# Seven block products for gate and up in the first feed-forward layer too, its down product in five groups added by DMA, and a new order of the seven in both layers

## The chip, the cores and the metric

The kernel runs on one core of one Trainium2 chip. TensorE (PE) multiplies, VectorE (DVE), ScalarE (ACT) and GpSimd (POOL) work on tiles in the on-chip memory SBUF and on the accumulators in PSUM (eight banks of 2 KB per partition), and 16 DMA engines move data. DMAs are issued from queues of SyncE (SP), ACT and POOL; only those from POOL's queue add to their destination here (`accum_op=OP.add`). The metric is the device time of one execution in microseconds (us), as the median of several runs. Matmuls are written in float32 in two parts, see below.

## The reference

One inference step of a trunk of two layers over 576 tokens (512 of a prompt, 64 of a sample group), model width 1024. Each layer is a mixer and a gated feed-forward part, both behind an RMS norm and added to the residual x. Layer 0 mixes by dilated sliding-window attention, layer 1 by a diagonal complex state-space scan with a GLU. The part that matters here, the same in both layers:

```python
D_FF = 2816
def swiglu(h, w_gate, w_up, w_down):
    return (jax.nn.silu(h @ w_gate) * (h @ w_up)) @ w_down

h2 = rmsnorm(x, p['norm_ffn'][i])
x = x + swiglu(h2, p['ffn_w_gate'][i], p['ffn_w_up'][i], p['ffn_w_down'][i]).astype(x.dtype)
```

The outputs are the two residual streams, the updated key and value caches (most of which is a copy of the old cache, shifted by 8 positions) and the states of the scan.

## The kernel before

**Tiles.** x lives transposed in SBUF as `xT`: 8 tiles of 128 model rows by 576 tokens. A matmul takes 128 by 128 weights and 288 tokens (HN), half of the tokens. Every float32 operand is split in two, hi (fp32r, a rounded copy made on ACT, tile `whi` or `xgh`) and lo (the rest, a subtraction on DVE, `wlo` or `xgl`), and a product is three matmuls: hi by hi, hi by lo, lo by hi. `split_w` (line 95) splits a weight tile of 512 KB (`raw`, four k-tiles by 256 columns), `mm6` (line 105) issues the six matmuls of three terms and two token halves.

**Stages in order of time.** The qkv projection with attention over the caches (to about 397 us of the span); the output projection (`wo_phase`), four chunks of 256 columns, each followed by the residual addition on DVE and by `Norm.add`, which splits the new tile for the next layer part and adds its squares to `ssum` (ACT squares, POOL adds); the first feed-forward layer (`ffn`, 423 to 868 us); the state-space part (`ssm_phase`) with its GLU (to about 1065 us); the second feed-forward layer (`ffn_last`).

**First feed-forward layer, `ffn`.** 11 units of 256 columns. A unit computes its gate chunk directly, 2 halves of columns x 8 k-tiles x 6 matmuls, multiplies by the norm's factor `r` on DVE (L1078), takes silu on ACT (L1079), multiplies by r again on POOL (L1080); then the same for up, and the product of both (L1085) is split to `hh` and `hl` (L175, L176). After 4, 8 and 11 units (`THIRDS`) the down product of these units is computed in four chunks of 256 columns of the model width, and DVE adds it into `xT` (L1091). After each chunk of weights `tick()` runs a piece of `fill`: `ssm_setup` is a generator that computes the constants of the state-space layer (powers, tables, masks; mostly DVE and POOL with some transposes on PE) and writes them to DRAM scratch; its last pieces load the first four sets back.

**Second feed-forward layer, `ffn_last`.** Gate and up of a unit are taken together as one product with a 2 by 2 block structure: weights a11 to a22 (row halves by k halves, prepared on the host in `w_gu`; each block is 128 partitions by 4 k-tiles by 256 columns), activations b11 to b22 (k halves by token halves). Seven products of sums of blocks replace eight (line 1097):

```python
PRODUCTS = (("a11", "b11"), ("s1", "t1"), ("a12", "b21"), ("s2", "t2"), ("s3", "t3"), ("a22", "t4"), ("s4", "b22"))
```

s1 and s3 are made by DMA: a block is loaded through SP's queue, and a second one added to it from POOL's queue (`plus`, L1127). s2 is s1 + a11 on DVE (L1156), and becomes s4 by one more `plus`. The t operands are sums of the b, made with their splits in `Norm7.add` (lines 235 to 256) during the GLU: seven hi and seven lo parts per pair of tiles of x, four sums on DVE (L244, L249, L251, L253). The products accumulate in three pairs of banks (x, y and z in `products`); between two products that use the same bank, ACT or DVE copies the partial sum out (`ended`, L1178 `cp`, L1182 `cq`). Weights of the next unit are fetched when s3 of the present one is split.

**Queues.** SP issues loads and cache copies in program order. The copies of the old cache into the outputs (`shifts`, 88 of about 1 MB, DRAM to DRAM) are paid out by `pace`: each weight load in the feed-forward layers with `rate=RF` = 1.0 adds one copy. The order of instructions on each engine is set by the framework's scheduler from the program order; where `keep_in_program_order` or `issue_after` stands, by hand.

## Time and profile before

| what | us |
| --- | --- |
| median of 3 runs (1469.40 to 1473.09) | 1471.54 |
| the profiled execution | 1472.93 |
| its span in the trace | 1471.1 |
| output projection, PE's last matmul ends about | 423 |
| first feed-forward layer | 423 to 868 |
| second feed-forward layer | 1066 to 1471 |

The mean granted clock of TensorE over the span is 0.994. A row of the group view reads: line, engine, operation, output <- inputs, shapes, count | busy time in us, mean of one in ns | idle time of the engine before it, and what ended that. Matmuls are pipelined, so their own durations (about 295 ns) overlap; how far apart they follow is read from the busy time of a stretch and the number of matmuls in it. A row of the view by stage gives busy time and number of instructions of PE, PE's weight loads, DVE, ACT and POOL, then the granted clock, the mean busy share of the 16 DMA engines and GB/s. [...]

### The profile page before, as it was taken

To read this page: it belongs to the slowest core of one execution; us is meant where nothing else is said; L and a number is where in the kernel's file an instruction comes from. 1 tells how busy PE (TensorE), PEld (TensorE's weight loads), DVE (VectorE), ACT (ScalarE), POOL (GpSimd) and SP (SyncE) were. 2 spreads that over 40 slices of the span, in tenths; PEclk is the share of its full clock that TensorE was granted. 3 is DMA by queue.
4 is the path that set the end of the run, shared out by engine and by line. 5 is a ranking of instruction groups with operands and counts; after the bars stand their busy time and mean duration, and the time that the engine had idled before them with its cause. 6 is when DMAs were issued, how large, how long until landed. Compare 5 with 4: busy or idle time off the path is not lost. (4 is left out here: it accounts for less than half of the span.)

```text
span 1471.1 us, 30038 instructions
## 1 busy us (share of the span) xinstructions
PE 1432.1 (97%) x12398; PEld 1341.1 (91%) x12398; DVE 1000.9 (68%) x1696; ACT 596.0 (41%) x962; POOL 334.6 (23%) x410
## 2 busy tenths in 40 slices
PE   9999999999999999999999999699999999999998
PEld 7888777777899999999999999699999999999998
DVE  5898989745578653687777567856587646755772
ACT  4534455465462221223123363434365324532541
POOL 2022131320031066156245330131010001100110
PEclk9999999999999999999999999899999999999999
DMA  7566798999897757888979857964267767775532
GB/s 243 207 232 234 224 306 278 347 307 330 301 298 257 264 216 270 300 298 313 318 269 319 290 178 227 275 181 130 86 169 190 242 216 184 184 244 156 146 110 63
DMA packets 181048, 345.73 MB, mean 235 GB/s; under 512 B 40720, under 2 KB 116304, under 8 KB 179504
## 3 DMA queue, kind: packets, MB, share of 16 engines
q1 hardware_dynamic: 168176, 309.00, 61.4%
q0 software_dynamic: 9968, 32.12, 9.8%
q10 hardware_dynamic: 2768, 2.70, 0.6%
q8 instruction: 97, 1.59, 0.4%
q14 instruction: 39, 0.32, 0.1%
HBM read 312.29 MB, written 118.78 MB: 293 GB/s over the span
## 5 line engine op out<-in xcount | busy, mean ns | idle before, releaser
L108 PE MATMUL acc<-xgh,wlo 128*128 128x288 f32 x1056 | 227.6, 297 | 3.4 <-DVE wlo L100 3.4
L108 PE MATMUL acc<-xgh,whi 128*128 128x288 f32 x1056 | 229.5, 299 | 0.0
L108 PE MATMUL acc<-xgl,whi 128*128 128x288 f32 x1056 | 227.3, 297 | 0.0
L99 ACT ACTIVATE whi<-raw 128x1024 fp32r<-128x1024 f32 x98 | 102.0, 1041 | 242.8 <-PE acc L108 193.9
L1171 PE MATMUL bank<-xoh,whi 128*128 128x288 f32 x616 | 182.5, 296 | 4.2 <-ACT cq L1182 2.8
L1171 PE MATMUL bank<-xoh,wlo 128*128 128x288 f32 x616 | 181.7, 295 | 0.2 <-DVE wlo L1113 0.2
L1171 PE MATMUL bank<-xol,whi 128*128 128x288 f32 x616 | 181.7, 295 | 0.0
L108 PEld LDWEIGHTS acc<-xgh,wlo 128*128 128x128 f32 x1056 | 170.6, 189 | 4.0 <-DVE wlo L100 3.9
L108 PEld LDWEIGHTS acc<-xgh,whi 128*128 128x128 f32 x1056 | 170.3, 189 | 1.8 <-issue 1.2
L108 PEld LDWEIGHTS acc<-xgl,whi 128*128 128x128 f32 x1056 | 170.5, 189 | 0.1
L100 DVE TENSOR_TENSOR wlo<-raw,whi 128x1024 fp32r<-128x1024 f32 x98 | 124.7, 1272 | 67.3 <-ACT whi L99 66.3
L1171 PEld LDWEIGHTS bank<-xoh,whi 128*128 128x128 f32 x616 | 115.7, 188 | 6.1 <-ACT cq L1182 4.4
L1113 DVE TENSOR_TENSOR wlo<-raw,whi 128x1024 fp32r<-128x1024 f32 (+1 forms) x57 | 70.7, 1241 | 73.3 <-ACT whi L1112 73.3
L384 PE MATMUL acc<-whi,xh 128*128 128x512 f32 x288 | 118.7, 414 | 1.6 <-ACT xh L324 1.5
L1171 PEld LDWEIGHTS bank<-xoh,wlo 128*128 128x128 f32 x616 | 115.8, 188 | 0.6 <-DVE wlo L1113 0.6
L1171 PEld LDWEIGHTS bank<-xol,whi 128*128 128x128 f32 x616 | 115.7, 188 | 0.1
L1112 ACT ACTIVATE whi<-raw 128x1024 fp32r<-128x1024 f32 (+1 forms) x57 | 58.4, 1029 | 136.6 <-DMA raw<-ffn_w_down 52.1
L384 PE MATMUL acc<-wlo,xh 128*128 128x512 f32 x288 | 112.2, 391 | 0.0
L384 PE MATMUL acc<-whi,xl 128*128 128x512 f32 x288 | 111.5, 393 | 0.0
L108 PE MATMUL acc<-hh,whi 128*128 128x288 f32 x352 | 76.2, 297 | 0.0
L1080 POOL TENSOR_TENSOR gt<-gt,rstd 128x576 f32<-128x576 f32 x22 | 39.4, 1794 | 160.5 <-ACT gt L1079 160.4
L1127 POOL DMA_DIRECT2D s<-w_gu x22 | 19.4, 883 | 247.3 <-DMA s<-w_gu 145.5
(445 smaller groups left out, 3142.5 us busy)
## 6 DMA issues: line engine op xcount, KB each, us to landing
o_kv_s<-cache_kv_w SPq DMA_DIRECT2D x64, 1020.0 KB, 7.7
kc<-cache_kv_w SPq DMA_DIRECT2D x100, 512.0 KB, 6.9
raw<-ffn_w_down SPq DMA_DIRECT2D x40, 512.0 KB, 3.8
raw<-w_qkv SPq DMA_DIRECT2D x36, 512.0 KB, 7.0
raw<-w_gu SPq DMA_DIRECT2D x33, 512.0 KB, 3.4
kc<-qscr SPq DMA_DIRECT2D x32, 512.0 KB, 6.1
o_kv_s<-cache_kv_w SPq DMA_DIRECT2D x16, 1008.0 KB, 7.5
raw<-ffn_w_gate SPq DMA_DIRECT2D x22, 512.0 KB, 5.1
```

What stands on the lines that cost most here:

```text
L99: s.activation(hi, raw, AF.Copy)
L100: mark[0] = v.tensor_tensor(lo, raw, hi.bitcast(F32), OP.subtract)
L108: pem[0] = te.matmul(ps[:, c, :HN], w, x[:, c * HN:(c + 1) * HN], start=first and i == 0, stop=last and i == 2)
L384: ins = nc.tensor.matmul(*a, **kw)
L1080: g.tensor_tensor(t, t, nin.r, OP.mult)
L1112: s.activation(hi, raw, AF.Copy)
L1113: v.tensor_tensor(lo, raw, hi.bitcast(F32), OP.subtract)
L1127: g.dma_start(fl(t), block(c, m, k), accum_op=OP.add)
L1171: tc.keep_in_program_order(te.matmul(acc[q][:, :HN], a[:, k, i * 128:(i + 1) * 128], nin.x[x, k][b], skip_group_check=n != "a12", start=n ...
```

## The change

- `ffn_last` becomes `ffn` for both layers (argument `layer`), so the first layer too computes gate and up in seven block products. The host now prepares `w_gu` for both layers. The first layer has 6 PSUM banks for it (the other two stay with `aux` for the set-up), one buffer each for s1 and s3 instead of two (`1 + layer`), s2 in a `raw` buffer, and 4 for `hh`/`hl`. For the first unit its s2 is made by DMA.
- The norm ahead of the first layer (`n0`) becomes a `Norm7`: `wo_phase` makes seven split operands per pair of tiles; those of the last pair come after all residual additions. The norm's last step is computed after the first three k-tiles of three products, and partly on POOL.
- The new order of the seven, in both layers: a11, a12, s2, s1, s3, s4, a22. s1's partial sum is copied out by ACT; s3 and s4 are added to such copies by DVE.
- The first layer's down product is computed in five groups of units, (2, 2, 2, 2, 3); the first four are computed after the first product of the next unit, evicted by ACT, and added to `xT` by a DMA from POOL's queue. The last group is added on DVE.
- The cache copies are paid out otherwise: 11 in the attention part (`SHIFTS`), 0.2 per split and 0.5 per down load in the first layer, some 16 in the GLU, 0.3 and 0.5 in the second layer.
- `ssm_setup` is cut into more and smaller pieces; several copies and the masks go from DVE to ACT, one step of powers from POOL to DVE, and the loads of its first four sets of constants move into `ssm_phase`, onto SP's queue.
- The attention output's hi parts (`ath`) lie in four buffers of `kst`, and pools are opened and closed at other places.

```diff
-RF = 1.0
+SHIFTS = (4, 5, 6, 7, 10, 11, 15, 16, 17, 18, 19)
+RF = 0.5
...
-            v.tensor_tensor(t, self.r, self.r, OP.mult)
-            v.tensor_tensor(t, t, m, OP.mult)
+            e = v if self.perm else g
+            e.tensor_tensor(t, self.r, self.r, OP.mult)
+            e.tensor_tensor(t, t, m, OP.mult)
...
-                v.scalar_tensor_tensor(self.r, t, 1.5, self.r, op0=OP.add, op1=OP.mult)
+                g.tensor_scalar(t, t, 1.5, None, op0=OP.add)
+                g.tensor_tensor(self.r, t, self.r, OP.mult)
...
-    n0 = Norm(1)
+    n0 = Norm7(1, xo)
...
-            n0.add(2 * c + m)
+            if c < 3:
+                n0.add(f)
+    n0.add(6)
+    n0.add(7)
...
+PRODUCTS = (("a11", "b11"), ("a12", "b21"), ("s2", "t2"), ("s1", "t1"), ("s3", "t3"), ("s4", "b22"), ("a22", "t4"))
+GROUPS = (((0, 2), (2, 4), (4, 6), (6, 8), (8, 11)), ((0, 4), (4, 8), (8, 11)))
+PACE = (0.2, 0.3)
+FETCH = ("a11", "s1", "a12", "s3", "a22")
...
+    bk = es.enter_context(tc.tile_pool(name=f"bk{layer}", bufs=8 if layer else 6, space=PSUM))
...
+    def fetch(c, n):
+        if n[0] == "a":
+            W[c][n] = load(c, "12".index(n[1]), "12".index(n[2]), ring, "raw", 4)
+        else:
+            W[c][n] = load(c, 1, 0, r7, n, 1 + layer)
+            plus(W[c][n], c, *{"s1": (1, 1), "s3": (0, 0)}[n])
...
+            if n == "s3":
+                if c + 1 < 11:
+                    fetch(c + 1, "a11")
+                if tail:
+                    fetch_down(*tail, 0)
+                if c + 1 < 11:
+                    for i in FETCH[1:] if not tail else ("s1", "s3"):
+                        fetch(c + 1, i)
...
+            pace(PACE[layer])
+            tick()
...
+            elif n in ("s1", "s2"):
+                s.activation(t[i][n == "s1"][:, 1], p, AF.Copy)
+            elif n in ("s3", "s4"):
+                d = t[i][n == "s3"][:, 1]
+                v.tensor_tensor(d, p, d, OP.add)
...
+        for n, x in rest:
+            ready(n)
+            for i in range(2):
+                products(n, x, i, range(4))
+            if n == "a11" and mid is not None:
+                down(*mid, False)
...
+                if not end:
+                    y = wk.tile([128, 2, HN], F32, name=f"{'gu'[c % 2]}t{m}")
+                    for q in range(2):
+                        if layer:
                             v.tensor_tensor(y[:, q], ps[m][q][:, :HN], nin.r[:, q], OP.mult)
+                        else:
+                            s.activation(y[:, q], ps[m][q][:, :HN], AF.Copy)
+                    if layer:
                         v.tensor_tensor(xv, y, xv, OP.add)
+                    else:
+                        g.dma_start(xT[:, f, :], y.rearrange("p a b -> p (a b)"), accum_op=OP.add)
+                    continue
...
-                tt = wk.tile([128, 8, 16, 8], F32, name="wo")
-                v.tensor_tensor(tt.rearrange("p g c t -> p t (g c)"), st, tmask[:, :, None].to_broadcast([128, 8, 128]), OP.mult)
+                for t in range(8):
+                    s.activation(tt.rearrange("p g c t -> p t (g c)")[:, t], st[:, t], AF.Copy, scale=tmask[:, t:t + 1])
...
+    consts_in(0, nc.sync)
     stage1(0)
     fetch1(2)
+    consts_in(1, nc.sync)
     stage1(1)
...
+            with tc.issue_after(L["mark"][0].ins):
+                L["pace"]((0.0, 1.75, 1.75, 1.0 if c0 >= D else 0.0)[c0 % D // 256])
```

599 lines of the change are left out of this document (319 added, 280 removed).

## The prediction

> **What bounds the kernel now.** I read the page's busy times first, then the list of what TensorE (PE) waits for, then the busy times by stage.
>
> ```profile
> span 1471.1 us, 30038 instructions
> PE 1432.1 (97%) x12398; PEld 1341.1 (91%) x12398; DVE 1000.9 (68%) x1696; ACT 596.0 (41%) x962; POOL 334.6 (23%) x410
> ...
> PE acc L1646 <- DMA U<-u_scr: 11.6, 2, 10.9
> ...
> PE bank L1171 <- ACT cq L1182: 2.8, 6, 0.8
> PE bank L1171 <- ACT sq L198: 1.4, 1, 1.4
> ```
>
> PE is busy for 97% of the span, and of its waits by far the largest is 11.6 us in stage 2 of the state-space part; the seven products of the second layer wait 2.8 and 1.4 us. So the kernel is as long as its queue of matmuls, and a matmul removed in a stage without waits is time removed, provided that nothing else becomes late there. In the next view each row is a stretch: busy time and instructions of PE, weight loads, DVE, ACT, POOL, then granted clock, DMA share, GB/s.
>
> ```profile
> 403.00:423.00 20.00, 20.00 (x152) 20.00 (x151) 17.41 (x33) 12.32 (x18) 7.91 (x6) 1.00 1.01 264
> 423.00:868.00 445.00, 442.55 (x3411) 438.98 (x3410) 303.60 (x566) 127.70 (x142) 179.41 (x148) 1.00 0.80 284
> 630.00:680.00 50.00, 50.00 (x401) 49.26 (x400) 41.58 (x64) 14.92 (x17) 27.06 (x16) 1.00 0.96 336
> ...
> 1090.00:1156.00 66.00, 65.36 (x487) 64.51 (x486) 46.52 (x60) 37.23 (x57) 7.77 (x9) 1.00 0.79 204
> ...
> 1252.00:1274.00 22.00, 22.00 (x168) 21.98 (x168) 15.75 (x20) 12.13 (x19) 2.59 (x3) 1.00 0.79 195
> ```
>
> 423 to 868 is the whole first feed-forward layer: PE 442.55 of 445 us. The last row holds exactly one unit of the second layer (seven products, 168 matmuls) without a gap: 22.00 / 168 = 131 ns per matmul of 288 columns. That is the price of a matmul in what follows.
>
> **The saving.** Gate and up of one unit of 256 columns take 192 matmuls now (2 matrices x 2 halves of columns x 8 k-tiles x 3 terms x 2 halves of tokens), and 7 x 2 x 4 x 3 = 168 in the new form. 24 x 11 units = 264 matmuls, x 131 ns = **-34.6 us**. The down product keeps its 1056 matmuls whatever its groups, and the set-up of the state-space layer, which runs in the gaps of this stage, keeps its transposes. In the second layer the new order puts two products instead of one between two that share a bank, so that the copy of an accumulator has 6.3 us of matmuls (48 x 131 ns) over it in place of 3.1 us: the 2.8 us of waits for cq should go, **-2.8 us**, at worst 0.
>
> **The late start.** The block products need seven split operands per pair of 128-row tiles in place of two wider ones, made in the output projection, which is short. Rows: DVE's residual adds, its low halves and sums, the weight split, and one of the sums that ran beside POOL.
>
> ```profile
> L1038 DVE TENSOR_TENSOR xT<-acc,xr 128x288 f32<-128x288 f32 (+1 forms) x16 | 9.2, 620 | 1.2 <-DMA xr<-x_scr 1.2
> L1038 DVE TENSOR_TENSOR xT<-acc,xr x16: 548/622/698, 403.4 to 423.7; 128x288 f32<-128x288 f32 x8, 128x224 f32<-128x224 f32 x8
> L100 DVE TENSOR_TENSOR wlo<-raw,whi 128x1024 fp32r<-128x1024 f32 x98 | 124.7, 1272 | 67.3 <-ACT whi L99 66.3
> L232 DVE SCALAR_TENSOR_TENSOR xol<-S,xoh 128x288 fp32r<-128x288 f32 x16 | 6.6, 444 | 0.0
> L232 DVE SCALAR_TENSOR_TENSOR xol<-xT,gm,xoh 128x288 fp32r<-128x288 f32 x12 | 6.1, 511 | 1.8 <-ACT xoh L231 1.8
> L199 POOL TENSOR_TENSOR ssum<-ssum,sq 128x576 f32<-128x576 f32 x21 | 35.7, 1701 | 137.1 <-ACT sq L198 137.1
> L1039 DVE TENSOR_TENSOR xT<-acc,xr x8: 209/218/237, 404.4 to 424.2; 128x64 f32<-128x64 f32 x8
> L249 DVE SCALAR_TENSOR_TENSOR S<-xT,gm,S x4: 1501/1676/1676, 994.2 to 1070.1; 128x288 f32<-128x288 f32 x4
> L251 DVE SCALAR_TENSOR_TENSOR S<-xT,gm,S x4: 504/506/508, 995.6 to 1071.7; 128x288 f32<-128x288 f32 x4
> ```
>
> From the first add, at 403.4 us, DVE has: adds 9.2 + 8 x 0.218 = 10.9 us; five weight splits (two of the projection, three of the first unit) x 1.27 = 6.4; low halves 16 x 0.41 + 12 x 0.51 = 12.7; sixteen sums x 0.506 = 8.1. That is 38 us. Durations overlap a little at their ends (the busy time of sixteen L232 is 6.6 us, not 7.1), so 34 us is possible; with seven POOL additions over it (L199), each lengthening one two-input instruction by 1.676 - 0.506 = 1.2 us as in L249, 46 us. DVE is therefore done at 437 to 450 us, and the operands of the last pair that the early products need come some 3 us before. PE ends the projection near 423, and has 54 matmuls of the first three pairs and the norm's two sums over, about 8 us, so until 431. Stall 434 - 431 = 3 us to 447 - 431 = 16 us; I take **+9 us**, the middle. Now there is no stall here (20.00 of 20 us busy, 403 to 423).
>
> [...]
>
> ```profile
> 940.00:950.00 10.00, 3.86 (x64) 3.89 (x66) 5.00 (x10) 2.40 (x8) 0.00 (x0) 0.50 1.04 293
> ```
>
> A PE gap lowers the granted clock here: it is 0.50 in the stretch of the 10.9 us wait. I price this at nothing beyond the gap itself, within the bounds above. [...]
>
> **The rest of the first layer.** Three resources get fuller. Rows of DVE and of the DMA queues, the first six in the stretch 423 to 868, the next four in three units of the second layer (1090 to 1156).
>
> ```profile
> L100 DVE TENSOR_TENSOR wlo<-raw,whi 128x1024 fp32r<-128x1024 f32 (+1 forms) x69 | 87.1, 1262 | 41.2 <-ACT whi L99 40.3
> L1562 DVE TENSOR_TENSOR wo<-st,tmask 128x1024 f32<-128x1024 f32 x8 | 17.7, 2218 | 0.3
> L1439 DVE COPY cwd<-cw 128x128 f32<-128x128 f32 x16 | 4.8, 297 | 4.8 <-PE aux L1440 4.8
> q1 hardware_dynamic: 53665, 125.78, 79.9%
> o_kv_s<-cache_kv_w SPq DMA_DIRECT2D x59, 1020.0 KB, 7.7
> o_kv_s<-cache_kv_w SPq DMA_DIRECT2D x4, 1008.0 KB, 9.6
> ...
> q0 software_dynamic: 1243, 4.50, 39.9%
> q1 hardware_dynamic: 2570, 8.90, 38.6%
> s<-w_gu SPq DMA_DIRECT2D x6, 512.0 KB, 4.9
> s<-w_gu POOLq DMA_DIRECT2D x6, 512.0 KB, 6.4
> ```
> ```profile
> L1078 DVE TENSOR_TENSOR gt<-acc,rstd 128x576 f32<-128x576 f32 x22 | 16.3, 750 | 6.4 <-PE acc L108 6.3
> L1085 DVE TENSOR_TENSOR ut<-acc,gt 128x576 f32<-128x576 f32 x22 | 16.6, 754 | 9.6 <-PE acc L108 8.9
> L1091 DVE TENSOR_TENSOR xT<-acc,xT 128x576 f32<-128x576 f32 x24 | 18.1, 756 | 22.1 <-PE acc L108 22.1
> L1200 DVE SCALAR_TENSOR_TENSOR ut<-ut,gt 128x576 f32<-128x576 f32 x22 | 16.5, 750 | 3.9 <-ACT ut L1184 2.3 <-POOL gt L1197 1.3
> L1194 DVE SCALAR_TENSOR_TENSOR gt<-gt,rstd 128x576 f32<-128x576 f32 x22 | 18.0, 818 | 0.1
> L1188 DVE TENSOR_TENSOR gt<-bank,cp 128x288 f32<-128x288 f32 x11 | 5.0, 450 | 0.0
> L1156 DVE TENSOR_TENSOR S<-s,raw 128x1024 f32<-128x1024 f32 x11 | 13.4, 1215 | 0.0
> L1112 ACT ACTIVATE whi<-S 128x1024 fp32r<-128x1024 f32 x22 | 23.4, 1061 | 21.0 <-PE bank L1171 11.9 <-DMA S<-w_gu 8.7 <-DVE S L1156 0.3
> ```
>
> DVE: 303.6 us now. Gone: 44 of the 69 splits (55.5), L1078 and L1085 (32.9), two thirds of L1091 (12, the down sums go by DMA, their eviction to ACT), the masks L1562 (17.7, to ACT) and some 70 small copies like L1439's that move to ACT or vanish (x 0.297, some 20). New: 77 splits x 1.26 = 97; ten S sums 12; 66 evictions with an addition x 0.45 = 30; 44 products with the norm, 18.0 + 16.5 = 35; some 8 us of powers taken from POOL and 14 us that the late start leaves behind 423. 165 + 196 = **361 us** in a stage of 445 - 34.6 = 410 us: 88%, against 68% now and 83% in the densest stretch quoted (41.58 of 50 us, with PE at 50.00).
>
> DMA: a plain MB costs 355.6 / 125.78 = 2.83 us of all 16 engines, an accumulating one 26.3 / 4.50 = 5.85 us; a unit of the second layer costs (26.3 + 25.5 - 2.9 for one cache copy) / 3 = 16.3 us. Now 355.6 us. Gone: 44 loads of gate and up (23.1 MB, 65 us; a few lie before 423, as the first unit's will), some 36 of 63 cache copies (they go to the attention part, the GLU and the second layer: 106 us), the constants' 7.3 MB (21). New: 11 x 16.3 = 179, and 32 additions of 0.295 MB into xT x 5.85 = 55 (this form is not in the trace; at the plain price it is 27). **370 to 398 us** over 410: 90 to 97%, against 80% now and 96% in the densest 50 us.
>
> So PE, DVE and DMA have nearly equal work. What hides the new work is only depth: weights split one or two products (3.1 us each) ahead. The longest chain is that of s1: load 4.9 us, POOL's issue and the accumulating load 6.4, the S sum 1.2 (L1156), the split on ACT and DVE 1.06 + 1.26, together 15 us; there are five products (15.7 us) plus the lead between the product that starts it and the one that needs S. It fits, by little; the second layer's order of before leaves the same chain four products, and PE's waits show nothing of it. A fetch or addition queued on POOL behind one that waits holds all of POOL's arithmetic, and those behind SP's cache copies (7.7 us to land) come later too. Cost: 0 if it goes as in the second layer (there 4.2 us of waits in eleven units with DVE at 46.5 / 66 = 70%), up to 25 us if DVE can do no more than its densest 83% (361 / 0.83 = 435 us, less 410). I take **+8 us**, nearer to the second layer because the same loop ran there. Cache copies moved into the attention part (11 x 3 us of DMA in a stretch with room) and the GLU: 0 to 3, **+1 us**.
>
> ```profile
> 40.00:170.00 130.00, 129.56 (x626) 105.48 (x625) 118.35 (x154) 58.33 (x89) 21.56 (x40) 1.00 0.62 214
> 990.00:1062.00 72.00, 72.00 (x544) 71.95 (x543) 44.99 (x59) 29.64 (x48) 7.23 (x5) 1.00 0.40 119
> ```
>
> The room is in these rows: DMA 62% and 40% busy. The GLU takes about 16 copies x 3 us in 72 us, which fills it. The wait for U (11.6 us) comes from the order on SP's queue, which now carries the constants' loads as well; it may vanish or double, 0 +-12, I take 0.
>
> **Sum**, against the profiled execution's own 1472.9 us (span 1471.1 and 1.8 around it): -34.6 - 2.8 + 9 + 8 + 1 = -19.4, so 1453.5. That execution is 1.4 us over the median of the three runs (1471.5), so **1452 us** as a median. This kernel's times are told from no change at about 0.3%, 4.4 us.
>
> **Rivals.**
> - *Nothing new is late* (0.12): operands are made in the order in which PE needs them, stall 3, later stalls 0: 1472.9 - 37.4 + 3 - 1.4 = 1437 us. For it: PE 50.00 of 50 with DVE at 83% and DMA at 96%. Against: all of it at once, for 400 us.
> - *DVE becomes the bound of the first layer* (0.20): 435 us there plus 3 of the late start not counted in it, in place of 445: -7, with the second layer's order -2.8, +1, or 1463 us; with worse bunching up to 1471. Half of this is within 0.3%. PE then does less work, as the change says, and waits for the difference.
> - *DMA becomes the bound* (0.15), the slower end: the stage's 398 us at a mean share of 0.85, which lies between today's 0.80 and the densest 0.96, take 468 us, 23 more than now: 1472.9 + 23 - 2.8 - 1.4 = 1492 us. It decides from a mean share below 398 / 448 = 0.89. Against it: stretches of 0.96 and 1.01 above, with PE full.
> - The forecast (1443 to 1463): 0.53.
>
> Faster by over 0.3%: 0.53 + 0.12 + 0.11 = 0.76; within: 0.09; slower: 0.15. The range 1438 to 1480 leaves out half of the first rival and most of the third.
>
> **What would show it.** PE should have some 264 matmuls fewer; the first layer should last about 427 us. The late start shows as a wait of PE for DVE's or ACT's operands at 423 to 445 us; DVE as bound shows as many PE waits for split weights (wlo); DMA as bound as ACT's split waiting for raw or S with the DMA row at 9 throughout. The waits for cq in the second layer should be gone. The forecast is wrong if the late start exceeds 16 us, if waits inside the first layer sum to more than 25 us, or if the wait for U moves by more than its size.

## The result: 4.5% slower, and the profile after

| what | before | after |
| --- | --- | --- |
| median, runs of both beside each other, us | 1472.32 (1469.4 to 1475.51, 4 runs) | 1538.75 (1534.01 to 1544.52, 4 runs) |
| ratio of the times | | 1.0452, 95% interval 1.041 to 1.0495 |
| span of the profiled execution, us | 1471.1 | 1537.2 |

The change makes the kernel 66 us slower, where the prediction had 20 us faster and a range that ended at 1480. The page of the kernel after, in its first two parts:

```profile
span 1537.2 us, 30220 instructions
PE 1431.4 (93%) x12134; PEld 1330.9 (87%) x12134; DVE 1082.0 (70%) x1767; ACT 715.9 (47%) x1293; POOL 390.3 (25%) x461
...
PEclk9999999999979999999989999989999999999999
```

PE has 12398 - 12134 = 264 matmuls fewer, as the arithmetic of the seven products says, and yet it is busy for as long as before (1432.1 us then). So two things must have happened: matmuls became slower, and idle time appeared (97% of the span became 93%). The clock row (slices of 38.4 us) has its 7 and its first 8 in the first layer. The view by stage says where. First the kernel after, in stretches that begin and end where a stage does (columns as in the prediction), then the stages behind the first layer in the kernel before:

```profile
427.70:924.50 496.80, 435.63 (x3132) 424.10 (x3131) 380.41 (x633) 249.04 (x473) 226.86 (x194) 0.93 0.81 225
...
924.40:1129.50 205.10, 186.58 (x1931) 183.05 (x1931) 133.05 (x200) 83.09 (x151) 34.02 (x47) 0.96 0.87 285
1129.50:1531.20 401.70, 395.28 (x2941) 390.77 (x2942) 246.32 (x323) 168.44 (x251) 44.37 (x41) 1.00 0.68 208
```

```profile
867.20:1066.80 199.60, 184.70 (x1922) 181.26 (x1921) 133.31 (x198) 83.67 (x157) 33.61 (x47) 0.97 0.58 172
...
1066.80:1465.20 398.40, 394.62 (x2943) 390.10 (x2943) 245.80 (x326) 170.53 (x251) 36.81 (x37) 1.00 0.62 175
```

The first layer grows from 445.0 to 496.8 us: +51.8 of the 66. The rest is small: the output projection ends at 427.7 instead of about 423 (+4.7), the state-space part and GLU take about 6 us more, the second layer 3.3 us more, although it got the better order.

The 51.8 us can be split further. Before, PE's idle time in the stage was 445.00 - 442.55 = 2.5 us; now it is 496.80 - 435.63 = 61.2 us, **58.7 us more idle**. At the matmul price of before PE would have been busy for 442.55 - 34.6 = 408 us; it is busy for 435.6, so there are **27.7 us of slow matmuls**. 58.7 + 27.7 - 34.6 = 51.8. The saving is there in full, and is outweighed two and a half times.

What ended the idle time shows in PE's waits in this stage (us in total, times, longest):

```profile
PE bank L1251 <- DVE hl L186: 10.7, 6, 2.9
PE bank L1188 <- DVE wlo L1101: 9.9, 8, 2.8
PE bank L1188 <- ACT whi L1100: 7.8, 2, 5.5
PE bank L1251 <- ACT hh L185: 7.1, 3, 4.3
PE bank L1188 <- ACT xoh L243: 6.3, 1, 6.3
PE aux L1629 <- ACT wo L1621: 6.2, 3, 3.9
PE bank L1188 <- DVE gt L1202: 4.9, 2, 3.4
PE bank L1188 <- DVE ut L1202: 4.8, 2, 3.5
```

L1188 are the seven products, L1251 the down product. No single wait carries the loss. PE waits for DVE and for ACT by turns, for split weights, evictions and the down product's operands, 2 to 6 us at a time; before, the same layer had one such wait:

```profile
PE acc L108 <- DVE wlo L100: 2.5, 1, 2.5
```

About 16 us of the idle time after lie in the first unit (6.3 us ahead of its first product, 5.5 ahead of its last, four small ones), the other 45 inside the layer.

How one such wait comes about is seen in the timeline of DVE (start, duration, instruction, in brackets the idle time ahead of it):

```profile
543.37 0.44 DVE L1202 TENSOR_TENSOR gt<-bank,gt 128x288 f32<-128x288 f32 x1
550.81 1.22 DVE L1159 TENSOR_TENSOR raw<-s,raw 128x1024 f32<-128x1024 f32 x1 [7.00 <-issue]
551.96 0.45 DVE L1202 TENSOR_TENSOR ut<-bank,ut 128x288 f32<-128x288 f32 x1
```

L1159 is the sum s2 = s1 + a11. It stood at the head of DVE's queue for 7.00 us, because the transfer that adds the second block to s1, issued at 541.0, landed only at 550.7. The eviction L1202 behind it did not pass it: its inputs were ready by 549.0, and it began at 551.96, 3 us later. PE ran out at the same place:

```profile
552.46 0.40 PE L1188 MATMUL bank<-xoh,whi 128*128 128x288 f32 x1 [3.50 <-DVE ut L1202]
```

The transfers, issue to landing, in the first layer of the kernel after:

```profile
s<-w_gu POOLq DMA_DIRECT2D x20, 512.0 KB, 9.6
s<-w_gu SPq DMA_DIRECT2D x19, 512.0 KB, 5.3
```

An accumulating load takes 9.6 us here, 6.4 in the three units of before's second layer that the prediction used. With L1159 at a mean of 1.52 us and wlo at 1.44 (before 1.26), the chain of s1 is 5.3 + 9.6 + 1.5 + 1.06 + 1.44 = 19 us, not 15, over five products that last 15.7: it does not fit.

The slow matmuls follow the gaps. Stretches of about 2 us around a wait of 2.14 us that ended at 819.26, and around one of 1.63 us that ended at 656.84:

```profile
815.00:817.00 2.00, 2.00 (x16) 1.89 (x15) 1.53 (x2) 0.00 (x0) 2.00 (x2) 1.00 1.06 295
817.00:819.20 2.20, 0.12 (x1) 0.00 (x0) 0.46 (x1) 1.02 (x2) 2.20 (x3) 1.00 0.90 321
819.20:821.00 1.80, 1.74 (x19) 1.33 (x20) 0.82 (x1) 1.23 (x3) 0.97 (x3) 0.51 1.08 200
821.00:823.00 2.00, 2.00 (x11) 2.00 (x11) 1.59 (x2) 0.00 (x0) 1.92 (x3) 0.59 1.00 317
823.00:825.00 2.00, 2.00 (x18) 2.00 (x16) 0.00 (x0) 0.74 (x2) 0.99 (x1) 1.00 0.91 134
...
656.80:659.00 2.20, 2.16 (x16) 2.16 (x17) 2.20 (x4) 0.09 (x1) 0.00 (x0) 1.00 0.97 171
```

Behind the longer one the granted clock (third number from the end) is 0.5 from 819.2 to 822.6, 3.4 us; behind the shorter one it stays 1.00. So this gap of 2 us cost nearly 4. Length alone does not decide, though. Behind a longer wait, of 2.76 us, the clock stays 1.00:

```profile
670.71 0.40 PE L1188 MATMUL bank<-xoh,wlo 128*128 128x288 f32 x1 [2.76 <-DVE wlo L1101]
```

```profile
667.90:670.70 2.80, 0.05 (x1) 0.00 (x0) 2.80 (x2) 0.00 (x0) 2.72 (x3) 1.00 1.03 274
670.70:675.90 5.20, 4.95 (x47) 4.52 (x48) 5.17 (x6) 2.85 (x5) 5.04 (x3) 1.00 1.02 346
```

What does is seen in the trace's record of the granted clock. All its changes in this kernel fall on one grid of 3.41 us. Among the stretches of this grid at full clock, each with 1.83 us or more of idle PE was followed by one at half the clock, and none with 1.67 us or less was; full clock came back only after a stretch with at most 0.33 us idle. In the kernel before, whose changes lie on such a grid too, 2.42 us did and 1.84 us did not. The wait of 2.14 us lies almost wholly in one stretch (2.11 us of it); the one of 2.76 us is divided by a line of the grid at 669.0 into 1.1 and 1.7 us.

### The profile page after: what moved, and what is told of

Its sections match the earlier page's. It is cut to its first block, busy times and chain, and to the rows that moved or that the text cites. A ratio compares the mean times of both kernels' runs of the same rounds, so it can differ in the third digit from the quotient of the medians.

```text
span 1537.2 us, 30220 instructions
## 1 busy us (share of the span) xinstructions
PE 1431.4 (93%) x12134; PEld 1330.9 (87%) x12134; DVE 1082.0 (70%) x1767; ACT 715.9 (47%) x1293; POOL 390.3 (25%) x461
## 5 line engine op out<-in xcount | busy, mean ns | idle before, releaser
L1188 PE MATMUL bank<-xoh,whi 128*128 128x288 f32 x1232 | 373.5, 303 | 29.3 <-ACT whi L1100 9.3
L1188 PE MATMUL bank<-xoh,wlo 128*128 128x288 f32 x1232 | 372.3, 302 | 12.7 <-DVE wlo L1101 12.6
L1188 PE MATMUL bank<-xol,whi 128*128 128x288 f32 x1232 | 370.8, 301 | 1.1 <-DVE xol L244 1.1
L1188 PEld LDWEIGHTS bank<-xoh,whi 128*128 128x128 f32 x1232 | 238.9, 194 | 33.5 <-ACT whi L1100 9.9
L1101 DVE TENSOR_TENSOR wlo<-raw,whi 128x1024 fp32r<-128x1024 f32 (+1 forms) x136 | 182.0, 1339 | 103.2 <-ACT whi L1100 103.0
L1188 PEld LDWEIGHTS bank<-xoh,wlo 128*128 128x128 f32 x1232 | 238.5, 194 | 16.9 <-DVE wlo L1101 16.8
L1188 PEld LDWEIGHTS bank<-xol,whi 128*128 128x128 f32 x1232 | 238.6, 194 | 1.5 <-DVE xol L244 1.4
L1251 PE MATMUL bank<-hl,whi 128*128 128x288 f32 x352 | 85.8, 309 | 10.7 <-DVE hl L186 10.7
L1251 PE MATMUL bank<-hh,whi 128*128 128x288 f32 x352 | 84.7, 309 | 7.2 <-ACT hh L185 7.1
L1251 PE MATMUL bank<-hh,wlo 128*128 128x288 f32 x352 | 83.9, 306 | 0.0
L109 PE MATMUL acc<-xgl,whi 128*128 128x288 f32 x352 | 75.6, 295 | 2.3 <-DVE xgl L1694 2.3
L109 PE MATMUL acc<-xgh,whi 128*128 128x288 f32 x352 | 75.2, 298 | 0.9 <-ACT whi L100 0.9
L1251 PE MATMUL bank<-xgh,wlo 128*128 128x288 f32 x352 | 75.5, 295 | 0.5 <-DVE wlo L1101 0.5
L109 PE MATMUL acc<-xgh,wlo 128*128 128x288 f32 x352 | 75.2, 295 | 0.3 <-DVE wlo L101 0.2
L1251 PE MATMUL bank<-xgh,whi 128*128 128x288 f32 x352 | 75.3, 295 | 0.0
L1251 PE MATMUL bank<-xgl,whi 128*128 128x288 f32 x352 | 75.0, 294 | 0.0
## 6 DMA issues: line engine op xcount, KB each, us to landing
o_kv_s<-cache_kv_w SPq DMA_DIRECT2D x64, 1020.0 KB, 10.5
```

Source lines behind the costliest of these rows:

```text
L109: pem[0] = te.matmul(ps[:, c, :HN], w, x[:, c * HN:(c + 1) * HN], start=first and i == 0, stop=last and i == 2)
L1101: v.tensor_tensor(lo, raw, hi.bitcast(F32), OP.subtract)
L1188: L["pem"][0] = tc.keep_in_program_order(te.matmul(acc[q][:, :HN], a[:, k, i * 128:(i + 1) * 128], nin.x[x, k][b], skip_group_check=n != " ...
L1251: L["pem"][0] = te.matmul(ps[m][q][:, :HN], w, x[:, q * HN:(q + 1) * HN], start=a + k + j == 0, stop=a + k == len(ks) - 1 and j == 2)
```

## The experiments

Three theories at first. **A**: the set-up of the state-space layer, which runs beside the units, makes the units late on shared queues. **B**: the transfers are late, by the single buffer for s1 or by the cache copies beside them. **C**: the down sums that go by DMA from POOL's queue hold POOL. "Stage" is from the first of the seven products of the first layer to its last down product: 434.0 to 924.0, 490.0 us, in the kernel after. Except for the two repairs (4 runs) and the new order alone (12 runs) each kernel below ran once. The four runs of the whole change lie 10.5 us apart, so a difference of 6 or 8 us is a single reading, not more.

**All set-up ahead of the units.**

```diff
-    n1 = ffn(nc, tc, A, L, 0, n0, ssm, sp)
+    for _ in ssm:
+        pass
+    n1 = ffn(nc, tc, A, L, 0, n0, iter(()), sp)
```

> The whole set-up of the state-space layer runs before the first unit of the first feed-forward layer, none of it beside the units. Read by stage, not by total (the set-up alone then stands in the open and costs 100 us or more). Changed kernel: first product to last down matmul of the first layer 434 to 924, 490 us, of which PE idles some 55 and loses some 28 to a lower clock. Theory A (the set-up's arithmetic on POOL, ACT and DVE beside the units is what makes their operands late): the stage falls to 381 us of matmuls plus 5 to 25, 386 to 406 us, with PE waits under 20 us. Theory B (the loads and accumulating loads of the units' own weights are late, through one buffer for s1 and the cache copies): the stage stays above 440 us, with the waits for split weights as many as before. Theory C (the down sums by DMA on POOL's queue hold the others): above 440 us as well, waits at the group boundaries unchanged.

1675.85 us beside 1473.85 for before, since nothing covers the set-up now; but the stage itself takes 429.0 us. Its waits:

```profile
PE bank L1190 <- DVE ut L1204: 18.2, 4, 6.3
PE bank L1190 <- ACT cp L1197: 10.2, 1, 10.2
PE aux L1646 <- DVE kk L1638: 0.7, 1, 0.7
PE bank L1253 <- DVE hl L186: 0.3, 1, 0.3
```

The waits for hl, hh, wlo and wo are gone. What is left is one gap at the start and four at the sum of s1. The accumulating loads of s1 and s3 take 10.8 us even here, so it is not the set-up that makes them slow. So set-up matters, and is not all.

**No cache copies in the first layer** (they go to the second).

```diff
-PACE = (0.2, 0.3)
+PACE = (0.2, 0.65)
...
-            pace(PACE[layer])
+            pace(PACE[layer] if layer else 0.0)
```

The down weights' rate becomes 0 in the first layer as well.

> No cache copies are paid out in the first feed-forward layer; the second layer takes them (0.65 per split instead of 0.3). Theory B with the copies as its cause: loads land sooner (5.3 to about 4 us, accumulating ones 9.6 to about 7), the stage falls from 490 to 430 to 450 us and the total by 40 to 60 us. Theory A or C: the stage stays within 15 us of 490, total within 15 us of 1538 (the second layer may lose a few us).

The stage takes 481.3 us, 9 less, where theory B with the copies as its cause had 40 to 60; the accumulating loads land in 7.7 us. But the whole is 1582.5 us, 44 slower than the change: the second layer, which now has the copies, went from 402 to 458 us. There, one row of the transfers and one of PE's waits:

```profile
S<-w_gu POOLq DMA_DIRECT2D x11, 512.0 KB, 15.3
```

```profile
PE bank L1188 <- ACT whi L1100: 40.4, 9, 8.0
```

The addition that turns S2 into S4 lands in 15.3 us there, against 9.4 in the kernel after and 5.5 in the version with the new order alone (below), and PE waits for its split. The share of DMA is 0.76 in this layer as a mean, but the mean hides when. While ten of these eleven additions were under way (11.8 to 19.8 us each) it was 0.80 to 1.01; it was 0.62 during the eleventh, which landed in 5.4 us. One of the ten and the eleventh:

```profile
1293.60:1309.90 16.30, 15.94 (x121) 15.70 (x119) 7.88 (x12) 4.71 (x7) 0.87 (x1) 1.00 0.96 298
1512.10:1517.50 5.40, 5.40 (x43) 5.40 (x42) 4.17 (x6) 3.17 (x5) 2.32 (x2) 1.00 0.62 97
```

So the cache copies were no filler without a price: the single transfer on the chain was late while the share was 0.80 or more, whatever the mean of 0.76 says.

**Down sums on DVE instead of by DMA.**

```diff
-                        g.dma_start(xT[:, f, :], y.rearrange("p a b -> p (a b)"), accum_op=OP.add)
+                        v.tensor_tensor(xv, y, xv, OP.add)
```

> The down sums of the first four groups are added into the residual by DVE from the evicted copy (32 additions of about 0.75 us) instead of by DMA from POOL's queue. Theory C: the stage falls from 490 to 450 us or less, accumulating weight loads land in about 7 us. Theories A and B: within 15 us of 490, or longer by up to 24 us because DVE has more to do.

1537.28 us, stage 488.9: no difference, though DVE is busy for 20 us more (393.88 of 488.9):

```profile
431.10:920.00 488.90, 436.38 (x3131) 425.18 (x3131) 393.88 (x651) 245.06 (x468) 214.06 (x158) 0.92 0.70 206
```

Theory C falls, and this is a first sign that DVE's busy time isn't what counts. Nor is it the sum of the transfers: the DMA share falls from 0.81 to 0.70, which is 55 us less, and the stage is as long.

**A second buffer for s1 in the first layer.**

```diff
-            W[c][n] = load(c, 1, 0, r7, n, 1 + layer)
+            W[c][n] = load(c, 1, 0, r7, n, 2 if layer or n == "s1" else 1)
```

Room for it comes from laying short-lived tiles of the set-up over each other.

> Two buffers for s1 in the first layer instead of one (room made by laying three small tiles of the set-up over others). Theory B with the single buffer as its cause: DVE no longer waits 5 to 7 us for s1 ahead of the S sum, the stage falls from 490 to 440 to 460 us, total by 30 to 50 us. Theories A and C: within 15 us of 490.

1529.68 us, stage 478.2, 12 less. The waits for gt and ut fall from 9.7 to 2.0 us; hl (11.4), wlo (11.1), wo (7.0) and hh (6.8) stay. The 7.8 us of waits for whi are gone as well, which are not waits at the sum: 5.5 of them stood ahead of the first unit's last product, where the addition that makes s4 landed 12.3 us after its issue at 456.30, and now lands 5.4 us after 452.32. The waits for cp rise to 4.6. So the 12 us are not the chain of s1 alone.

**Both: set-up ahead and two buffers for s1.**

> All set-up ahead of the units, as in the run of that kind, and a second buffer for the block S1 in the first layer. There the layer's products and down product took 429 us against about 381 us of matmuls at full clock: 28.9 us idle, 18.2 of them in four waits for an eviction that stood on DVE behind a sum waiting for S1, and about 19 us of slow matmuls. Theory B (the chain over the one S1 buffer is what is left, and the slow matmuls come with its gaps): the four waits go, and with them about two thirds of the slow matmuls; the stage takes 400 to 412 us. Theory A (set-up alone, S1 only waits for something else): within 6 us of 429. Rival D (the accumulating loads are late whatever the buffers are, because the DMA engines are full, 81% there): 418 to 429 us, the waits moved to other blocks.

The stage takes 395.9 us, less than theory B hoped for. The row of its stretch, of the kind shown above:

```profile
634.30:1030.20 395.90, 391.89 (x2909) 390.81 (x2909) 240.94 (x279) 201.62 (x330) 117.32 (x103) 0.99 0.85 235
```

All four waits at the sum are gone, with the matmuls' slowness. It also corrects the price in the expectation: full-clock matmuls are about 390 us here, not 381, so that the set-up's own are 408 - 390 = 18 us. Now the parts can be priced. The second buffer is worth 12 us beside the set-up and 33 without it (429.0 to 395.9). With two buffers, the set-up costs 478.2 - 395.9 = 82 us, 18 of them its own matmuls: **64 us are interplay**. And PE is at 99% here with DMA at a mean share of 0.85, so such a share need not hold the products up. This stage is without the set-up's transfers, however. With them it has 0.81 x 490 = 397 us of DMA, which would be 0.96 of the 414 us that are hoped for; whether the stage could be as short as that with all its transfers, no run here shows.

**What of the set-up does it?** Four kernels on this. In the first, POOL's arithmetic for the table V is left out, and zeros are stored in its place.

```diff
-                for i, (a, b, op) in enumerate(((c1, c2, OP.add), (c2, c1, OP.subtract))):
-                    g.tensor_tensor(vv[:, i], a, p1r, OP.mult)
-                    g.tensor_tensor(vt_, b, p1i, OP.mult)
+                for i in range(2):
+                    g.memset(vv[:, i], 0.0)
                     yield
-                    g.tensor_tensor(vv[:, i], vv[:, i], vt_, op)
```

> Leaves out the six POOL operations that compute the recurrence's V table in each of its eight steps (48 operations, 79 us of POOL in the first layer) and stores zeros of the same size in its place. Theory L (POOL and DVE exclude each other: the differences wlo average 1.44 us in the first layer against 1.24 before, and single ones took 5.19 us beside these operations): wlo falls to 1.30 us or less, the first layer's stage from 490 to 465 to 478 us. Rival (DVE has room, what counts are the waits of DVE and ACT for transfers): wlo falls as well but the stage stays within 6 us of 490. Third: POOL issues the accumulating loads sooner, whatever DVE does: their issue to landing falls from 9.5 us to below 8.

1537.85 us, stage 488.3: nothing. The accumulating loads land no sooner either (10.0 us). A wlo does take longer beside POOL's arithmetic all the same. In the first layer of the kernel after, those with none beside them took 1.21 to 1.24 us, and one beside POOL's operations in a row 5.19:

```profile
665.46 5.19 DVE L1101 TENSOR_TENSOR wlo<-raw,whi 128x1024 fp32r<-128x1024 f32 x1 [2.00 <-ACT whi L1100]
```

```profile
665.31 1.72 POOL L1599 TENSOR_TENSOR st<-Cr,Ar 128x512 f32<-128x512 f32 x1
666.68 1.67 POOL L1599 TENSOR_TENSOR st<-Cn,Ar 128x512 f32<-128x512 f32 x1
668.02 1.54 POOL L1602 TENSOR_TENSOR st<-st,vt 128x512 f32<-128x512 f32 x1
```

and the groups of wlo, in the kernel after and without V's arithmetic:

```profile
L1101 DVE TENSOR_TENSOR wlo<-raw,whi 128x1024 fp32r<-128x1024 f32 x78 | 112.4, 1443 | 48.7 <-ACT whi L1100 48.5
```

```profile
L1101 DVE TENSOR_TENSOR wlo<-raw,whi 128x1024 fp32r<-128x1024 f32 x78 | 98.9, 1269 | 67.1 <-ACT whi L1100 66.9
```

The mean falls from 1443 to 1269 ns, DVE's work by 31 us, and all of it comes back as idle time of DVE, more than half as waiting for ACT (48.5 to 66.9 us for this group alone). Theory L is right that wlo gets shorter without these operations, and wrong about the time.

In the second, the table T has a tile of its own, so that ACT's next copy out of PSUM (`wo`) no longer waits for T's store.

```diff
-                tt = wk.tile([128, 8, 16, 8], F32, name="wo")
+                tt = wk.tile([128, 8, 16, 8], F32, name="tt")
```

> The table T of the recurrence gets a tile of its own, so that ACT's copy of the next block out of PSUM no longer waits for the store of the table before (16.2 us in the first layer, most of it in three waits). Room for it comes from laying short-lived tiles over each other. Theory A2 (ACT, held by that store, makes the units late): the waits of PE for this copy (6.2 us) and some of those for whi and hh go, the stage falls by 8 to 20 us to 470 to 482. Rival (ACT would have waited for PE there anyway): within 5 us of 490.

1537.45 us, stage 482.8. PE's waits for wo are gone, those for whi and hh as large as before: 7 us, between the two expectations, and the whole is no faster, within what one run can tell.

In the third, the set-up starts after the fourth block of the first unit.

```diff
-            if not 1 < ticks[0] < 5:
+            if ticks[0] > 4:
```

> The recurrence's set-up starts after the fourth block of the first unit, where its first step went ahead of that unit. Its ten loads then stand behind the unit's loads in SP's queue. Theory S (the late start is these loads ahead of the unit's own): the 5.5 us gap at the fifth block and the first gap shrink, the first unit ends 6 to 12 us sooner, and the stage is 480 to 485 us. Rival (the start waits for the norm's statistics and for buffers of w_o, not for the queue): the first unit within 3 us of where it was, the stage 485 to 495.

1531.46 us, stage 484.2. The gap that the expectation puts at the fifth block shrinks from 5.49 to 2.66 us, the first one from 6.28 to 5.03, all gaps of the first unit together from 16.2 to 13.2: as far as one run tells, the loads in SP's queue explain a fifth of the late start. The first down product begins at 498.8 instead of 502.8 us, 4 us sooner, between the two expectations. The gap of 5.49 us stands ahead of the unit's last product (144 of its 168 matmuls are done), and what is late there is not a plain load but the addition that makes s4. In the kernel after, POOL issues it only behind two operations of the norm's last step, which the change gave to POOL:

```profile
451.32 2.41 POOL L226 TENSOR_TENSOR sq<-sq,rs_m 128x576 f32<-128x576 f32 x1
453.82 2.51 POOL L232 TENSOR_SCALAR sq<-sq 128x576 f32<-128x576 f32 x1
456.30 0.89 POOL L1115 DMA_DIRECT2D raw<-w_gu  x1
```

In the fourth, on top of the two s1 buffers, DVE's table arithmetic is left out: the six products and sums of the powers and the eight shuffles of each of the eight steps; fills stand in their place.

```diff
-                for i, (b0, b1, op) in enumerate(((Br, Bi, OP.subtract), (Bi, Br, OP.add))):
-                    v.tensor_tensor(wt[:, 0], bw_(b0), rv(Ar), OP.mult)
-                    v.tensor_tensor(wt[:, 1], bw_(b1), rv(Ai), OP.mult)
-                    v.tensor_tensor(wr[f][:, i], wt[:, 0], wt[:, 1], op)
...
+                v.memset(wr[f], 0.0)
...
-                    v.stream_shuffle(st[:, t], kt, m)
+                v.tensor_copy(st[:, 0], kt)
+                v.memset(st[:, 1:], 0.0)
```

> On the version with two S1 buffers (stage 478.2 us, 45.5 of them idle). Leaves out what DVE computes in the recurrence's eight table steps: the six products and sums of the powers and the eight shuffles of each step; one fill and one copy of the same tiles stand in their place, so that the stores, POOL's and ACT's part and PE's remain. That takes some 58 us of DVE's 379 away. Theory F (the set-up's operations stand ahead of the units' evictions and splits in DVE's queue, and the group boundaries, where PE waits for hh and hl, feel it): the waits of PE for hl, wlo and gt fall from 27 us to below 10, the stage to 440 to 458 us. Rival G (it is the transfers that DVE and ACT wait for in their queues, not DVE's work; taking 62 us of work off POOL and 31 off DVE moved the stage by 2 us): 466 to 478 us.

1505.45 us. The row of the stage:

```profile
431.00:887.20 456.20, 425.12 (x3131) 415.03 (x3131) 330.14 (x468) 246.92 (x468) 220.03 (x189) 0.96 0.85 240
```

478.2 to 456.2: 22 us, at the slow end of theory F. PE's wait for hl falls from 11.4 to 4.8 us, for wlo from 11.1 to 8.1, for gt from 2.0 to nothing; together 12.9, less of a fall than F expected. Taking 49 us of DVE's work away here gives 22 us; taking 31 away by leaving out V's arithmetic gave 2 (there with one s1 buffer, whose waits may have hidden more). So it isn't DVE's total; what counts, it seems, is what stands ahead of an eviction or a split at the moment when PE needs it, and batches of powers and shuffles do.

**One masked copy on ACT instead of eight**, on the two s1 buffers (the table T is then not masked as it should be).

> On the version with two S1 buffers (stage 478.2 us). One copy on ACT stands in place of the eight masked copies of each table step (64 operations, 22.7 us of ACT); its other copies and the store of the table stay. Theory G2 (ACT is late: behind these copies and behind the store that its next copy waits for stand the units' whi and hh): PE's waits for whi, hh and wo fall, the stage to 462 to 472 us. Rival (ACT at 51% of the stage has room): 474 to 480 us.

1522.94 us, stage 472.2: 6 us, at the edge of theory G2. If one run is enough to tell, ACT's queue counts as well, with less.

**All of it light**: two s1 buffers, the late start of the set-up, and the arithmetic of V, of the masks and of DVE's tables left out. PE's transposes, the copies and the stores remain.

> On the version with two S1 buffers and without DVE's table arithmetic (stage 456.2 us): leaves out POOL's V arithmetic and seven of eight masked copies on ACT as well, and starts the set-up after the fourth block. What remains of the table steps is PE's transposes and small products, the copies out of PSUM, and the stores. Alone these three gave 2, 6 and 6 us. Theory F2 (the set-up costs by what stands in the queues of DVE and ACT, whichever operations): the gains add up, 436 to 446 us. Rival R (what remains is the waits of PE, ACT and DVE for the set-up's transposes and stores): 448 to 456 us.

1496.3 us, stage 446.7 (432.0 to 878.7). 9.5 of the 14 us that the three gave alone: between the two, nearer to the adding up. Against 395.9 + 18 = 414, 33 us stay, some 22 of them more idle time and 11 slower matmuls; the first wait of 7.6 us, now for the last residual addition on DVE, lies ahead of the stage and is not among them. So of the 64 us of interplay 22 + 9.5 are traced to what was left out or begun later, and half stays open: what the other waits are made of (cp, wlo, hl, wo, 3 us at a time) wasn't separated further. Even so the kernel would be slower than before.

**The repairs that keep the computation**: two s1 buffers and the late start.

> The whole change with two repairs that keep the computation: a second buffer for S1 and the set-up started after the fourth block. Alone they gave 12 and 6 us. If they are independent: the stage 470 to 474 us and 1520 to 1526 us in all, still 50 us slower than before. If the start's gain came from the S1 chain: 478 and 1530.

1518.64 us beside 1470.76, a ratio of 1.0329 (1.028 to 1.0378); stage 469.1. The gains add up (12 and 6 alone, 21 together), and are not enough.

**The new order alone**, second layer of the kernel before.

```diff
-PRODUCTS = (("a11", "b11"), ("s1", "t1"), ("a12", "b21"), ("s2", "t2"), ("s3", "t3"), ("a22", "t4"), ("s4", "b22"))
+PRODUCTS = (("a11", "b11"), ("a12", "b21"), ("s2", "t2"), ("s1", "t1"), ("s3", "t3"), ("s4", "b22"), ("a22", "t4"))
...
-                if n in ("a11", "s3"):
+                if n == "a11":
...
-                elif n == "s2":
-                    s.activation(cp[1][i], p, AF.Copy)
+                elif n in ("s1", "s2"):
+                    s.activation(t[i][n == "s1"][:, 1], p, AF.Copy)
+                elif n in ("s3", "s4"):
+                    d = t[i][n == "s3"][:, 1]
+                    v.tensor_tensor(d, p, d, OP.add)
...
```

> The kernel before with one part of the change: the new order of the seven products in the second layer, with S1's and S2's results copied out by ACT and the third and fourth sums added to them; the first layer stays in three products. The prediction gave this part 2.8 us, the two kinds of waits for the cp and cq copies; in the whole change these went and some 5 us of waits for weights stood in their place. Theory P (the part is worth its 2.8 us alone): 1468 to 1470.5 us beside 1472. Rival (new waits for splits take it back, as in the whole change): 1471 to 1477 us.

1467.82 us (12 runs) beside 1471.47 (17 runs), a ratio of **0.9967 (0.9952 to 0.9982)**: faster than both kernels, by 2.6 to 7.1 us. The stretch of its second layer, beside the 398.4 us of before:

```profile
1063.40:1459.90 396.50, 393.22 (x2943) 389.81 (x2943) 249.20 (x326) 170.40 (x251) 37.94 (x37) 1.00 0.62 177
```

The profiled layer is only 1.9 us shorter. The waits for cq are gone, but 2.6 us of waits for other copies of accumulators stand in their place, and PE's idle time goes from 3.8 to 3.3 us. So the gain is clear of noise, and its cause is seen only in part. In the whole change the same layer takes 401.7, with 3.1 us more idle time than here; the additional copies, beside which S<-w_gu lands in 9.4 us instead of 5.5, fit as the reason, but were not separated.

**Gaps on purpose.** On that last version, DVE repeats the difference that makes wlo of s3 fourteen times in every unit of the second layer, so that PE waits there.

```diff
                 hl[n] = split_w(w[n])
+                if n == "s3":
+                    for _ in range(14):
+                        v.tensor_tensor(hl[n][1], w[n], hl[n][0].bitcast(F32), OP.subtract)
```

> Prices the clock's after-effect by itself, in the second layer, where PE hardly ever waits: on the kernel before with the new order there, whose second layer from first product to last down product took 396.5 us with 3.3 us idle and 393.2 us of matmuls. Each of its eleven units gets fourteen repeats on DVE of the difference that makes wlo of S3 (some 17 us a unit), so that PE waits once or twice a unit for DVE; PE's work stays the same. The idle time should be 30 to 60 us. Theory K (a gap of several us is followed by some 8 us at half clock, as in the traces of the whole change): the matmuls' time rises by 30 to 60% of the idle time, to 405 to 425 us, and the profile's row shows half the clock behind the gaps. Rival (the slow matmuls of the whole change come from the load of the chip or from the transfers, not from the gaps): 393 to 396 us.

The idle time came out far longer than meant, PE's wait being eleven times some 16 us:

```profile
1062.10:1667.90 605.80, 418.18 (x2943) 413.20 (x2943) 434.76 (x481) 170.51 (x251) 38.01 (x37) 0.84 0.41 116
```

```profile
PE bank L1174 <- DVE wlo L1160: 186.2, 11, 21.9
```

The same 2943 matmuls take 418.18 instead of 393.22 us: **25 us more with nothing changed but gaps**, so the gaps are what slows the clock, not the load of the chip (DMA is at 0.41). But theory K had it by the share of idle time, and that is wrong: eleven gaps of 16 us cost 2.3 us each, no more than gaps of 2 to 6 us do. The price is per gap, as a mean:

| kernel | idle, us | gaps over 2 us | slow matmuls, us | each | PE busy at half clock, us |
| --- | --- | --- | --- | --- | --- |
| after | 54.5 | 14 | 27.5 (435.5 - 408) | 2.0 | 54.8 |
| two s1 buffers | 45.5 | 12 | 24.7 (432.7 - 408) | 2.1 | 49.3 |
| and no DVE tables | 31.1 | 7 | 17.1 (425.1 - 408) | 2.4 | 33.5 |
| set-up ahead | 28.9 | 5 | 10.1 (400.1 - 390) | 2.0 | 23.7 |
| gaps on purpose | 187.6 | 11 | 25.0 (418.2 - 393.2) | 2.3 | 52.3 |

The gap ahead of the first product is counted in the first three rows, though its idle time lies outside the stage. The last column is taken from the trace's record of the clock alone, and half of it is within 2 us of the slow matmuls in every row. So the half clock accounts for them all.

## Why the prediction was wrong

Its own warnings name the place ("if waits inside the first layer sum to more than 25 us"), and two of its counts held: PE lost 264 matmuls, and the demand on the engines came out near what it had worked out, 380 us of DVE against 361, and DMA 0.81 x 496.8 = 402 us against 370 to 398. The time went wrong by these steps:

- **The rest of the first layer, "I take +8 us", bounds 0 to 25: the step that failed.** Measured: about 45 us idle behind the first unit. Its ceiling was a busy share, "if DVE can do no more than its densest 83%". DVE was at 77% (380.4 of 496.8) and never the limit: 20 us more of work moved nothing (down sums), 31 us less hardly anything (V), while 49 us less at the right places gave 22. The ceiling should have been latency. What stood behind a waiting instruction in the queues of DVE and ACT waited too: the eviction behind the sum s2 began 3 us after its inputs were ready, and a split on ACT, ready by 464.3, began at 469.6, behind one that had waited 10.3 us for its transfer. The first layer puts both the set-up's batches and waits for transfers into these queues, and each hit passes on to PE once the lead of one or two products is used up. "Nearer to the second layer because the same loop ran there" left out what differs: in the second layer nothing else runs on these queues. With the set-up out of the way and two s1 buffers the loop did run like that, 4.0 us idle in the layer.
- **"It fits, by little"**: 15 us of the s1 chain over 15.7 us of products. The durations were those of the second layer with two buffers; beside the set-up, with one, the chain is 19 us. A second buffer was worth 12 us beside the set-up (not all of it by this chain), 33 without it. The comfort taken from the second layer of before was a misreading, too: there the sum s2 is needed after six products (s3, a22, s4, a11, s1, a12); what has four is s1's own split, without the sum. A margin of 0.7 us should have been priced as a loss, since the same text put DMA's demand up by a fifth.
- **"I price this at nothing beyond the gap itself"**: the clock's after-effect is 27.7 us in this layer, the largest single error of principle. The prediction quoted a row at half the clock, for a wait of 10.9 us. Measured were 2.0 to 2.4 us per gap of over 2 us, as a mean, with 14 such gaps here; a wait of 2.14 us was enough and one of 2.76 us was not, by where they lay on the grid. The kernel before had shown that a short wait can be enough, behind its one of 2.5 us in this layer:

```profile
596.30:599.70 3.40, 3.40 (x16) 3.40 (x16) 2.31 (x4) 1.68 (x3) 0.92 (x1) 0.50 1.31 461
```

- **The late start, +9 (3 to 16)**: 16.2 us of gaps in the first unit, at the upper bound, but not by the path worked out; that the size fits the bounds is partly luck. The prediction let PE run the first three pairs until 431 and then wait for the last one. PE waited 6.3 us before its first product: the profile names ACT's hi part here, and in six of the other kernels the last residual addition on DVE, which ends at 433.9 in this one. Not foreseen was the addition that makes s4 (5.5 us), late behind the norm's last step on POOL and 12.3 us in landing.
- **The second layer's order, -2.8**: right in size alone (2.6 to 7.1 us), lost in the whole change. By mechanism it is half right, as the waits for cq went and others came. The cover was also miscounted: between s2, s3 and a22, which share a bank, a copy has 36 matmuls over it instead of 12 (4.7 us for 1.6), not 48 for 24. "Cache copies moved, +1" didn't look at the second layer's own share of the copies, nor at the attention part, where PE's waits for cached keys rose from 2.5 to 5.1 us.
- **The wait for U, 0 +-12**: 7.8 instead of 11.6 us, within its bounds.
- **The rivals.** "DVE becomes the bound" and "DMA becomes the bound" both took one resource as full throughout. DVE had room, and taking 55 us of transfers away changed nothing; DMA was near full by turns, and late transfers fall into those turns (in the run with the copies in the second layer, a share of 0.80 to 1.01 while ten late additions were under way). The one that came true wasn't on the list: no engine is the bound, and the chain through all of them is. It was in the text as a remark ("what hides the new work is only depth"), without a price.

## What to carry to other kernels

When a loop is moved to a place where other work shares its queues, price the longest chain with the durations of that place and count every instruction that may stand ahead of its links in a queue; DVE's busy share, 77% here, said nothing about that. Look at the transfers' share while a transfer on that chain is under way, not at its mean over the stage. Where PE has run without gaps, count the gaps of over 2 us that a change adds and take, from the five kernels of the table, 2 us of slow matmuls for each as a mean, beside the gap. Try the parts of a large change alone: here the new order alone was worth 0.3%, hidden in a change that cost 4.5%.

## What the runs showed of the hardware that was not expected

- The granted clock changed on a grid of 3.41 us: in the kernel after, 1.83 us or more of idle PE within one stretch at full clock brought half the clock for the next, 1.67 us or less did not (in the kernel before 2.42 us did, 1.84 us did not). So one wait of 2.14 us halved the clock and one of 2.76 us, across a line of the grid, did not. The mean price per gap was about the same for gaps of 2 to 6 us (2.0 to 2.4 us) and of 16 (2.3 us).
- One DVE subtraction of two SBUF inputs took 5.19 us instead of 1.22, beside operations of POOL that followed one another from 665.31 us on. Beside a single one no such subtraction (wlo) in the same layer took more than 2.89 us.
- The accumulating load that makes s4 in the second layer landed in 5.5 us (median) with the new order alone, in 9.4 in the kernel after, and in 15.3 with the first layer's cache copies beside it. The mean DMA share of that layer was 0.76; while the ten that took 11.8 us or more were under way it was 0.80 to 1.01.
